# A part of expert 0 computed for all tokens before the routing is known, and another order of the experts

## The chip, the cores and the metric

The kernel runs on one core of a Trainium2 chip. TensorE multiplies matrices, VectorE and ScalarE compute on elements, GpSimd does little here, and SyncE (SP) issues the large transfers from memory, which 16 DMA engines carry. Each engine works through its own instructions in their order and waits for others by semaphores. The metric is device time in microseconds (us) of one execution; the profile takes times within one execution from its first instruction.

## The reference

A network of two layers (gated token mixing, differential attention, pooling; then a feed-forward part), followed by a second network of two layers, on 256 tokens of 1024 numbers. The feed-forward part of layer 1 is a mixture of eight experts, of which each token uses two:

```python
def moe_ffn(x, router_w, w1, w3, w2):
    logits = (xt @ router_w).astype(F32)            # 256 tokens x 8 experts
    top_v, top_i = lax.top_k(logits, TOP_K)         # TOP_K = 2
    top_w = jax.nn.softmax(top_v, axis=-1)
    gates = jnp.sum(jax.nn.one_hot(top_i, N_EXPERTS, dtype=F32) * top_w[..., None], axis=1)
    y = jnp.zeros_like(xt)
    for e in range(N_EXPERTS):
        y = y + gates[:, e:e + 1].astype(x.dtype) * swiglu(xt, w1[e], w3[e], w2[e])
    return y.reshape(bn, s, d)

def swiglu(x, w1, w3, w2):
    return (jax.nn.silu(x @ w1) * (x @ w3)) @ w2    # w1, w3: 1024 x 3584; w2: 3584 x 1024
x = layer_norm(ALPHA * x + f, ln2_g[l], ln2_b[l])   # ahead of it: x = layer_norm(ALPHA * x + h, ln1_g, ln1_b)
```

All is float32. With the inputs that the reference draws, 51, 28, 134, 12, 80, 48, 37 and 122 tokens choose experts 0 to 7.

## The kernel before

Every float32 product is made of three: a number is split into a high part (rounded by ScalarE to fp32r, `wh` for weights) and a low part (the rest, by VectorE, `wl`), and high x high, high x low and low x high are summed in PSUM (`Acc.mm`, L84). Weights come in *units* of 1 MB (128 partitions x 2048): `unit` (L169) takes a landing buffer `raw`, sends the transfer from SP, and splits the tile (`split`, L165) into `wh` and `wl`, of which there are four buffers each. A landing buffer is free again when VectorE has made `wl`. Tokens stand as two tiles of 128; `to_feat` (L313) transposes a tile into the feature-major `xah`, `xal`.

Order: `block1` drains layer 1's mixer, whose end is `project` (L383). Its last three units are multiplied for token tile 0 and then for tile 1; after each tile `layer_norm` (L353) works on VectorE from the two PSUM banks `prj` (r, statistics, aggregate, r, reciprocal of a root from ScalarE, xn). Then comes `moe`: `route` (L805) computes the logits `lgT`, ranks them, counts the tokens of each expert by four products with a matrix of ones (`cum`), sorts the experts by count into *slots* (0 the largest), and leaves the slots' experts in `idi`. A value of it decides a branch on every engine (L1236) between two plans, `few` and `many`; a plan is taken as `few` if slot 0 has up to 192 tokens, slot 1 up to 128 and slot 6 up to 64. Only in the branch does SP know which expert's weights to fetch.

An expert works on gathered tokens: `place` builds one-hot matrices `g`, `gather` (L910) multiplies them with the tokens (32 products `ga`, 256 or 512 columns wide), and the results are copied into `ring`. A full tile holds 128 tokens and needs three products per block of weights, a half tile holds 64 with high and low part side by side and needs two. In the plan `few` the first round takes slots 0 (a full and a half tile), 7 and 6 (half tiles) side by side; slots 1 to 5 follow, one full tile each. For each of seven blocks of 512 inner columns (`f`) an expert takes two units of w1 (`lin`), two of w3, four transposes (`uT`) and two units of w2 (`y`): 42 units. `stream` loads two units ahead. At the end `finish` puts the sum back to the tokens (`sct`) and adds it to the accumulator `xn`.

Instructions are put in order by a scheduler at build time, which also reorders across these calls; what it made stands below.

## Time and profile before

| what | us |
|---|---|
| median of three runs (2356.47 to 2361.75) | 2357.88 |
| the profiled execution | 2355.55 |
| its span, first to last instruction | 2353.8 |
| layer 1's last projection product to the first expert product | 411.5 to 442.0 |
| experts | 442 to about 1450 |

Busy time is a share of the span by engine; TensorE's products are pipelined, so that one lasts 0.39 us by its record while the next begins 0.23 us after it. PEld is the loading of weights into TensorE. The clock is what the chip granted to TensorE, as a share of full speed. The page's second part cuts the span into 40 slices of 58.8 us.

### The profile page before, as it was taken

Reading aid. Unit: us, or ns where it says so; the run is one execution under the profiler, and the core shown is the slowest. Engines: PE = TensorE matmul, PEld = TensorE weight load, DVE = VectorE, ACT = ScalarE, POOL = GpSimd, SP = SyncE. Lnnn points to the kernel's source line nnn. Section 1 sums busy time; section 2 is a strip of 40 time slices with the busy share of each in tenths; the row PEclk is TensorE's granted clock in tenths of the full one; section 3 lists DMA queues with packets and bytes.
Section 4 is the critical chain, followed back from the end, with each engine's and each line's share of the span. In section 5 each row is a group of like instructions: output and inputs, shape, how many; then the busy total and the mean of one; then the engine's idle time right before and its main releaser. Section 6 shows DMA issues by size and latency. Waiting matters only on the chain. (4 is left out here: it accounts for less than half of the span.)

```text
span 2353.8 us, 29770 instructions
## 1 busy us (share of the span) xinstructions
PE 2272.1 (97%) x11444; PEld 1853.7 (79%) x11444; DVE 1765.4 (75%) x1907; ACT 1396.0 (59%) x1532; POOL 108.9 (5%) x154
## 2 busy tenths in 40 slices
PE   7999999799999989999999997999999999999998
PEld 6788887577777768888888886787888888888887
DVE  4665476798888998889888888897666459956653
ACT  5554354677777777676776765457555343764542
POOL 2100011000000000000000001000200001010000
PEclk9999999899999999999999999999999999999999
DMA  9556560699999999999999997643755553555552
GB/s 298 167 191 187 178 209 21 248 343 345 344 337 322 330 326 368 347 368 362 371 342 371 369 365 255 200 162 117 230 190 181 192 189 126 188 172 186 191 185 72
DMA packets 266968, 585.10 MB, mean 249 GB/s; under 512 B 10514, under 2 KB 21190, under 8 KB 266561
## 3 DMA queue, kind: packets, MB, share of 16 engines
q1 hardware_dynamic: 260880, 565.48, 68.4%
q0 software_dynamic: 5936, 17.64, 2.6%
q8 instruction: 91, 1.49, 0.3%
q14 instruction: 61, 0.49, 0.1%
HBM read 580.43 MB, written 2.64 MB: 248 GB/s over the span
## 5 line engine op out<-in xcount | busy, mean ns | idle before, releaser
L167 DVE TENSOR_TENSOR wl<-raw,wh 128x2048 fp32r<-128x2048 f32 (+2 forms) x532 | 1195.5, 2268 | 373.2 <-ACT wh L166 372.1
L166 ACT ACTIVATE wh<-raw 128x2048 fp32r<-128x2048 f32 (+2 forms) x532 | 990.2, 1891 | 383.8 <-PE lin L84 145.3
L950 PE MATMUL lin<-wh,ring 128*128 128x512 f32 x1680 | 556.0, 391 | 0.0
L950 PE MATMUL lin<-wl,ring 128*128 128x512 f32 (+1 forms) x1008 | 396.2, 393 | 3.7 <-DVE wl L167 3.3
L950 PEld LDWEIGHTS lin<-wh,ring 128*128 128x128 f32 x1680 | 315.4, 188 | 81.8
L950 PEld LDWEIGHTS lin<-wl,ring 128*128 128x128 f32 (+1 forms) x1008 | 171.4, 170 | 48.7 <-DVE wl L167 8.5
L84 PE MATMUL lin<-wh,hh 128*128 128x512 f32 x352 | 141.8, 403 | 0.0
L84 PE MATMUL lin<-wl,hh 128*128 128x512 f32 x352 | 138.4, 393 | 2.3 <-DVE wl L167 2.3
L84 PE MATMUL lin<-wh,hl 128*128 128x512 f32 x352 | 137.9, 393 | 0.1
L950 PE MATMUL y<-wl,uh 128*128 128x512 f32 x336 | 107.3, 400 | 3.4 <-DVE wl L167 3.4
L1442 DVE SCALAR_TENSOR_TENSOR ro<-conv,ro 128x256 f32<-128x256 f32 x240 | 105.4, 474 | 0.4
L950 PE MATMUL y<-wh,ul 128*128 128x512 f32 x336 | 104.2, 391 | 0.0
L950 PE MATMUL y<-wh,uh 128*128 128x512 f32 x336 | 104.1, 390 | 0.0
L84 PE MATMUL lin<-wh,h2h 128*128 128x512 f32 x256 | 101.1, 395 | 0.0
L84 PE MATMUL lin<-wl,h2h 128*128 128x512 f32 x256 | 99.9, 390 | 0.2
L84 PE MATMUL lin<-wh,h2l 128*128 128x512 f32 x256 | 99.3, 390 | 0.2
L84 PE MATMUL lin<-wh,xah 128*128 128x512 f32 (+1 forms) x240 | 87.4, 365 | 0.7 <-ACT xah L166 0.6
L84 PE MATMUL lin<-wl,xah 128*128 128x512 f32 (+1 forms) x240 | 86.6, 361 | 0.0
L84 PE MATMUL lin<-wh,xal 128*128 128x512 f32 (+1 forms) x240 | 86.4, 363 | 0.0
L166 ACT ACTIVATE uh<-uT 128x512 fp32r<-128x512 f32 x42 | 25.1, 598 | 99.3 <-PE uT L1004 99.3
L84 PEld LDWEIGHTS lin<-wl,hh 128*128 128x128 f32 x352 | 66.7, 190 | 16.1 <-DVE wl L167 3.2
L84 PEld LDWEIGHTS lin<-wh,hh 128*128 128x128 f32 x352 | 66.8, 190 | 15.6 <-issue 1.3
(548 smaller groups left out, 3812.5 us busy)
## 6 DMA issues: line engine op xcount, KB each, us to landing
raw<-in_moe_w SPq DMA_DIRECT2D x336, 1024.0 KB, 7.2
raw<-in_w_in SPq DMA_DIRECT2D x70, 1024.0 KB, 5.1
raw<-in_w_ff SPq DMA_DIRECT2D x64, 1024.0 KB, 5.2
raw<-in_ffn_w SPq DMA_DIRECT2D x32, 1024.0 KB, 5.1
raw<-in_w_out SPq DMA_DIRECT2D x12, 1024.0 KB, 8.0
raw<-in_w_branch SPq DMA_DIRECT2D x8, 1024.0 KB, 5.7
raw<-in_w_out SPq DMA_DIRECT2D x8, 512.0 KB, 7.4
raw<-in_w_branch SPq DMA_DIRECT2D x8, 512.0 KB, 6.3
```

The source lines that it names most:

```text
L84: nc.tensor.matmul(o, lhsT=lhsT, rhs=rhs, start=(self.i == 0 and self.fresh), stop=(self.i == self.n - 1), skip_group_check=True)
L166: self.nc.scalar.activation(h, src, AF.Copy)
L167: self.nc.vector.tensor_sub(l, src, h.bitcast(F32))
L950: nc.tensor.matmul(a.ap[:rows], lhsT=lhsT, rhs=u[part][:, kk, cs], start=(a.i == 0), stop=(a.i == a.n - 1), skip_group_check=True)
L1442: nc.vector.scalar_tensor_tensor(acc[:, f], uT[:, f, k:k + 256], cw[:, f, k:k + 1], acc[:, f], op0=OP.mult, op1=OP.add)
```

## The change

Expert 0 is taken out of the sorting and goes to slot 0 always; the others are sorted by count into slots 1 to 7. The first block of 512 inner columns of expert 0 is computed for all 256 tokens, without gathering, by a new function `everyone`: six units, below called a0, a1 (w1), b0, b1 (w3), c0, c1 (w2), with 24 products each. a0 is loaded inside the projection (`hook`), the rest in `moe` around the two halves of `route`. The result is added to the accumulator with expert 0's gate, 0 for tokens that did not choose it. Four units of the next block are sent for ahead of the branch (`landed`). Expert 0's other six blocks run on gathered tokens as the plan's first round; slot 1 (full and half tile), 7 and 6 follow, then slots 2 to 5. The bounds for `few` become 128 tokens for expert 0, and 192, 128 and 64 for slots 1, 2 and 6. Six landing buffers go round in a fixed turn, where before every third load took one of the large pool.

```diff
+    def raw(self):
+        if self.raws:
+            self.raws.append(self.raws.pop(0))
+            return self.raws[-1]
+        return self.pw.tile([128, 2048], F32, tag="raw", name="raw")
...
-        raw = (self.big("raw") if self.roomy and self.loads % 3 == 0 else
-               self.pw.tile([128, 2048], F32, tag="raw", name="raw"))
+        there = bool(self.landed)
+        raw = self.landed.pop(0) if there else self.raw()
...
         after[1, 1] = self.early
+        if self.hook:
+            after[0, 0] = self.hook
...
+        key = col(8)
+        nc.vector.tensor_copy(key, cnt)
+        nc.vector.tensor_scalar(key[:, 0:1], cnt[:, 0:1], 1024.0, None, op0=OP.add)
...
+        most = (self.cap, self.cap + 64, self.cap, 64)
+        for i, (slot, m) in enumerate(zip((0, 1, 2, 6), most)):
...
+        def load(name, q):
+            u[name, q] = self.unit(w[name], list(range(4 * q, 4 * q + 4)), 0, 512)
+
+        def up(name, t):
+            x = self.xt_tok(xt)
+            p[name, t] = Acc(self.bank("lin"), 24)
+            for q in range(2):
+                h, l = u[name, q]
+                for kk in range(4):
+                    xh, xl = x(4 * q + kk, t)
+                    p[name, t].mm(nc, xh, h[:, kk])
+                    p[name, t].mm(nc, xh, l[:, kk])
+                    p[name, t].mm(nc, xl, h[:, kk])
+            if name == "a":
+                s[t] = self.mid("sa")
+                nc.scalar.activation(s[t], p[name, t].ap, AF.Silu)
+            else:
+                nc.vector.tensor_mul(s[t], s[t], p[name, t].ap)
...
+        def down(q):
+            h, l = self.unit(w2, [2 * q, 2 * q + 1], 0, 1024)
+            for t in range(2):
+                if q == 0:
+                    y[t] = [Acc(self.bank("y"), 12) for _ in range(2)]
+                for kk in range(2):
+                    uh, ul = (z[:, 2 * q + kk] for z in s[t])
+                    for st, m in ((uh, h), (uh, l), (ul, h)):
+                        for c in range(2):
+                            y[t][c].mm(nc, st, m[:, kk, c * 512:(c + 1) * 512])
...
-        gate, pos, iota, idi = self.route(xt, rw)
+        load, up, turn = (everyone[k] for k in ("load", "up", "turn"))
+        everyone["xt"].extend(xt)
+        self.raws = [*(self.raw() for _ in range(4)), self.big("raw"), self.big("raw")]
+        load("a", 1)
+        up("a", 0)
+        tr1()
+        route = self.route(xt, rw)
+        next(route)
+        load("b", 0)
+        load("b", 1)
+        up("b", 0)
+        up("a", 1)
+        gate, pos, iota, idi = next(route)
...
+        turn(0)
+        up("b", 1)
...
+        turn(1)
+        for q in range(2):
+            everyone["down"](q)
+        for t in range(2):
+            for c in range(2):
+                o = acc[:, t, c * 512:(c + 1) * 512]
+                nc.vector.scalar_tensor_tensor(o, everyone["y"][t][c].ap, gate[t][:, 0:1], o, op0=OP.mult, op1=OP.add)
+        landed = []
+        for w in (w1, w3):
+            for q in range(2):
+                landed.append(self.raw())
+                nc.sync.dma_start(landed[-1].rearrange("p (k n) -> p k n", n=512),
+                                  w[0, 512 * q:512 * q + 512, 512:1024].rearrange("(k p) n -> p k n", p=128))
...
-                for f in range(7):
+                for f in range(es[0][5], 7):
...
+        few = [([(0, 0, False)], [one(0)]),
+               ([(1, 0, False), (1, self.cap, True), (7, 0, True), (6, 0, True)],
+                [[(1, (0, 1), None), (7, (2,), 0), (6, (3,), 1)]]),
+               ([(2, 0, False)], [one(2)]),
+               ([(3, 0, False), (4, 0, False)], [one(3), one(4, 1)]),
+               ([(5, 0, False)], [one(5)])]
```

What the scheduler made of it stands in the next rows, at three places. First VectorE in the norm of token tile 1, from its first bank to the low parts of tile 1. Before:

```order
L363 SCALAR_TENSOR_TENSOR r<-xn,prj 128x512
L365 BN_STATS st<-r 128x6
L167 TENSOR_TENSOR xal<-tr,xah 128x4x128 x2
L363 SCALAR_TENSOR_TENSOR r<-xn,prj 128x512
L167 TENSOR_TENSOR rwhl<-route,rwhl 128x8x8
L365 BN_STATS st<-r 128x6
L366 BN_AGGR mv<-st 128x2
L370 SCALAR_TENSOR_TENSOR r<-r,mv,gb 128x512
L373 RECIPROCAL mv<-mv 128x1
L370 SCALAR_TENSOR_TENSOR r<-r,mv,gb 128x512
L375 SCALAR_TENSOR_TENSOR xn<-r,mv,gb 128x512 x2
```

The same place after the change; the three rows that write wl are the splits of a1, b0 and b1, in this order:

```order
L371 SCALAR_TENSOR_TENSOR r<-xn,prj 128x512
L168 TENSOR_TENSOR wl<-raw,wh 128x2048
L168 TENSOR_TENSOR xal<-tr,xah 128x4x128 x2
L373 BN_STATS st<-r 128x6
L371 SCALAR_TENSOR_TENSOR r<-xn,prj 128x512
L168 TENSOR_TENSOR wl<-raw,wh 128x2048
L373 BN_STATS st<-r 128x6
L168 TENSOR_TENSOR wl<-raw,wh 128x2048
L374 BN_AGGR mv<-st 128x2
L378 SCALAR_TENSOR_TENSOR r<-r,mv,gb 128x512 x2
L381 RECIPROCAL mv<-mv 128x1
L168 TENSOR_TENSOR rwhl<-route,rwhl 128x8x8
```

Three splits of weights now stand inside the norm. Second, TensorE at the four products `cum` that count the tokens of each expert. Before, the last router products stand directly ahead of them:

```order
L839 MATMUL lgT<-xal,rwhl 8x128
L843 MATMUL lgT<-ident,route 128x16
L855 MATMUL cum<-route 128x16
L856 MATMUL cum<-route,one 128x8
L857 MATMUL cum<-route,one 128x8
L858 MATMUL cum<-route,one 128x8
L1234 TENSOR_LOAD idi
L1236 COMPARE_AND_BRANCH
```

After, the end of 48 products of b0, b1 (tile 0) and a0, a1 (tile 1) stands ahead, and the transposes and 24 products of b0, b1 (tile 1) behind:

```order
L84 MATMUL lin<-wh,xah 128x512
L84 MATMUL lin<-wl,xah 128x512
L84 MATMUL lin<-wh,xal 128x512
L869 MATMUL cum<-route 128x16
L870 MATMUL cum<-route,one 128x8
L871 MATMUL cum<-route,one 128x8
L872 MATMUL cum<-route,one 128x8
L1138 MATMUL uT<-ident,sa 128x128 x4
```

The branch of TensorE has moved behind the other 24 products, four transposes and the 48 products of c0 and c1. Third, VectorE at the branch. Before:

```order
L878 TENSOR_TENSOR route<-route 128x64
L879 TENSOR_REDUCE keep<-route 128x8
L1234 TENSOR_LOAD idi
L1236 COMPARE_AND_BRANCH
L1124 TENSOR_SCALAR g<-keep 128x128 x2
L1124 TENSOR_SCALAR g<-keep 128x64 x6
L1146 MEMSET g 128x192 x2
L929 CAST ring<-ga 128x128
```

After, with the adding of the four banks of c0 and c1 to the accumulator (L1186), and then the first gather and the splits of the four units sent for ahead:

```order
L896 TENSOR_REDUCE keep<-route 128x8
L1186 SCALAR_TENSOR_TENSOR xn<-y,keep,xn 128x512 x4
L1331 TENSOR_LOAD idi
L1332 COMPARE_AND_BRANCH
L1219 TENSOR_SCALAR g<-keep 128x128 x2
L1241 MEMSET g 128x128 x2
L950 CAST ring<-ga 128x256
L168 TENSOR_TENSOR wl<-raw,wh 128x2048 x2
L950 CAST ring<-ga 128x256 x3
```

The four additions have come ahead of the branch, and two splits between the first and the other copies of the gather.

## Rows read from the trace of the kernel before

**Rows 1.** The page: TensorE's busy time, and GB/s in the 40 slices.

```profile
PE 2272.1 (97%) x11444; PEld 1853.7 (79%) x11444; DVE 1765.4 (75%) x1907; ACT 1396.0 (59%) x1532; POOL 108.9 (5%) x154
GB/s 298 167 191 187 178 209 21 248 343 345 344 337 322 330 326 368 347 368 362 371 342 371 369 365 255 200 162 117 230 190 181 192 189 126 188 172 186 191 185 72
```

**Rows 2.** Windows: stretch, length, busy by engine, granted clock, DMA share, GB/s.

```profile
core 0: us, PE busy (x) PEld busy (x) DVE busy (x) ACT busy (x) POOL busy (x), PEclk, DMA share, GB/s
411.53:441.97 30.44, 15.63 (x83) 13.25 (x83) 21.57 (x91) 12.46 (x32) 4.20 (x8) 0.72 0.31 110
441.97:811.00 369.03, 360.48 (x1655) 268.11 (x1653) 325.60 (x243) 273.88 (x230) 0.00 (x0) 1.00 0.96 343
811.00:1450.00 639.00, 631.73 (x2883) 517.96 (x2882) 570.53 (x382) 453.40 (x333) 1.09 (x2) 1.00 0.97 354
450.00:460.00 10.00, 10.00 (x45) 7.68 (x44) 7.77 (x5) 7.63 (x7) 0.00 (x0) 1.00 1.04 399
```

**Rows 3.** Groups by form, TensorE, 441.97 to 1450: the largest group.

```profile
L950 PE MATMUL lin<-wh,ring 128*128 128x512 f32 x1680 | 556.0, 391 | 0.0
```

**Rows 4.** The chain that ended last, at 1786 us: start, us, what.

```profile
1786.26 10.90 PE lin L84 x48
1797.15 0.87 PE uT L1824 x8
```

**Rows 5.** Waits of the engines, 1000 to 1400: us in total, times, longest.

```profile
PEld lin L950 <- DVE wl L167: 1.6, 3, 0.5
```

**Rows 6.** Waits of the SP queue, 340 to 1500: us in total, times, longest.

```profile
SPq L191 <- DVE wl L167: 760.4, 303, 25.1
```

**Rows 7.** Timeline of TensorE: start, us, what, [idle before <- what ended it].

```profile
411.30 0.39 PE L84 MATMUL prj<-wh,yl 128*128 128x512 f32 x1
416.16 1.97 PE L320 MATMUL tr<-ident,xn 128*128 128x128 f32 x8 [4.47 <-DVE xn L375]
...
420.81 0.22 PE L839 MATMUL lgT<-xal,rwhl 128*8 128x128 f32 x1
...
433.28 1.19 PE L922 MATMUL ga<-g,xh 128*128 128x512 f32 x2 [7.18 <-DVE g L1146]
...
441.97 0.39 PE L950 MATMUL lin<-wh,ring 128*128 128x512 f32 x1
```

**Rows 8.** Timeline of VectorE in the same stretch.

```profile
411.73 0.69 DVE L363 SCALAR_TENSOR_TENSOR r<-xn,prj 128x512 f32<-128x512 f32 x1 [1.04 <-PE prj L84]
...
415.36 1.41 DVE L375 SCALAR_TENSOR_TENSOR xn<-r,mv,gb 128x512 f32<-128x512 f32 x2
...
426.13 0.17 DVE L862 COPY route<-cum 128x8 f32<-128x8 f32 x1 [1.97 <-PE cum L858]
...
430.73 0.22 DVE L879 TENSOR_REDUCE keep<-route 128x8 f32<-128x64 f32 x1
431.47 1.46 DVE L1124 TENSOR_SCALAR g<-keep 128x128 fp32r<-128x128 f32 x8 [0.52 <-DVE keep L879]
432.91 0.42 DVE L1146 MEMSET g<- 128x192 f32 x2
```

**Rows 9.** Timeline among the experts: additions to the accumulator, and a unit's two splits.

```profile
1105.16 2.72 DVE L1060 SCALAR_TENSOR_TENSOR xn<-sct,keep,xn 128x512 f32<-128x512 f32 x4
...
1112.95 1.92 ACT L166 ACTIVATE wh<-raw 128x2048 fp32r<-128x2048 f32 x1 [0.29 <-PE lin L950]
...
1126.32 2.29 DVE L167 TENSOR_TENSOR wl<-raw,wh 128x2048 fp32r<-128x2048 f32 x1 [1.00 <-ACT wh L166]
```

**Rows 10.** Timeline of ScalarE and TensorE at the end of layer 1's attention.

```profile
390.69 0.60 ACT L657 ACTIVATE aT<-aTp 128x512 f32<-128x512 f32 x1 [3.76 <-PE aTp L655]
391.18 0.59 ACT L166 ACTIVATE yh<-oT 128x512 fp32r<-128x512 f32 x1
...
395.78 0.33 PE L686 MATMUL oT<-ident,o 128*128 128x128 f32 x1 [0.98 <-DVE o L680]
```

**Rows 11.** Timeline of TensorE: a gather 256 columns wide among the experts.

```profile
725.07 0.63 PE L922 MATMUL ga<-g,xh 128*128 128x256 f32 x4
725.54 0.63 PE L922 MATMUL ga<-g,xl 128*128 128x256 f32 x4
```

More of the change, by code (lines that the diff above doesn't have):

```diff
@@ L180, in unit @@
         rv, hv, lv = (z[:, :m].rearrange("p (k n) -> p k n", n=n) for z in (raw, h, l))
-        if layout == "rows":
+        if there:
+            pass
+        elif layout == "rows":
             sv = src[:, c0:c0 + n].rearrange("(g k d) n -> g d k n", g=2, d=64)
@@ L929, in gather, with expert @@
                         nc.vector.tensor_copy(d[1][:, k0:k0 + per], pv[:, :, c0:c0 + n])
-    def expert(self, tiles, w, acc):
+    def expert(self, tiles, w, acc, first):
         nc = self.nc
@@ L1014, in work @@
                         inner = z.get("sum") is not None
-                        if q == 0 and (f == 0 or inner):
-                            st[i]["y"] = [Acc(self.bank("y"), (4 if inner else 28) * per[i]) for c in range(2)]
+                        if q == 0 and (f == first or inner):
+                            st[i]["y"] = [Acc(self.bank("y"), (4 if inner else 28 - 4 * first) * per[i]) for c in range(2)]
                         products(z, st[i][f], (2 * q, 2 * q + 1), u,
@@ L1064, in settle @@
             self.warm(AF.Sqrt, z[:, 0] if tiles[0]["half"] else z[0][:, 0])
-        return up, down, turn, finish, settle
+        return up, down, turn, finish, settle, first
     def stream(self, jobs, ahead=2):
@@ L1087, in stream, with everyone, turn @@
             then()
-    def moe(self, xt, rw, w1, w3, w2, g2, b2):
-        tc, nc = self.tc, self.nc
-        gate, pos, iota, idi = self.route(xt, rw)
+    def everyone(self, w1, w3, w2):
+        nc = self.nc
+        w = {"a": w1, "b": w3}
+        u, p, s, y, xt = {}, {}, {}, {}, []
+        def load(name, q):
[13 more added lines that the diff above has]
+                nc.scalar.activation(s[t], p[name, t].ap, AF.Silu)
+            else:
+                nc.vector.tensor_mul(s[t], s[t], p[name, t].ap)
+        def turn(t):
+            b = self.bank("uT")
+            for j in range(4):
+                nc.tensor.transpose(b[:, j * 128:(j + 1) * 128], s[t][:, j * 128:(j + 1) * 128], self.ident)
+            h, l = self.mid("uh", (128, 4, 128), dt=F32R), self.mid("ul", (128, 4, 128), dt=F32R)
+            self.split(h, l, b.rearrange("p (j c) -> p j c", c=128))
+            s[t] = h, l
+        def down(q):
[8 more added lines that the diff above has]
+                            y[t][c].mm(nc, st, m[:, kk, c * 512:(c + 1) * 512])
+        return dict(first=lambda: load("a", 0), load=load, up=up, turn=turn, down=down, y=y, xt=xt)
@@ L1151, in weights @@
         def weights(s):
+            if s == 0:
+                return [w[0] for w in (w1, w3, w2)]
             rv = index.get(s)
@@ L1216, in make @@
                                     zs[0]["sum"] = ysum[:, inner]
-                                es.append(self.expert(zs, weights(s), acc))
+                                es.append(self.expert(zs, weights(s), acc, int(s == 0)))
                             return es
```

43 lines of the change are left out of this document (22 added, 21 removed).

## Prediction

> **What bounds the kernel now.** I read the page's busy shares and 40 slices first [rows 1]. TensorE is busy for 97% of the span, and one slice stands out in the transfers: the seventh (353 to 412 us) moves 21 GB/s, because nothing of an expert can be fetched before the router has chosen it. The change works at this hole and at the experts behind it, so I cut that part into stretches [rows 2]. From the last product of layer 1's output projection to the first expert product there are 30.4 us, TensorE is busy in half of them, and its granted clock is 0.72. From there to 1450 us TensorE is busy 360.48 of 369.03 us and 631.73 of 639.00 us, at clock 1.00.
>
> Does TensorE really set the pace there, or do the transfers, which run at 343 and 354 GB/s [rows 2]? The experts need 4032 products of 512 columns (12 per full tile and 8 per half tile in each weight unit; the row with 1680 of them is the largest part) [rows 3]. The pitch of such products is 10.90 / 48 = 0.227 us where nothing waits [rows 4]. 4032 x 0.227 = 915 us; with gathers, put-backs, small transposes and 16 us of idle that fills the 1008 us to within 2%. In the 400 us from 1000 to 1400 TensorE's weight loads waited 1.6 us for a split weight [rows 5], while the SP queue held back 303 loads for 760 us until VectorE gave back a landing buffer [rows 6]. So the loads wait for TensorE's progress, not TensorE for the loads: the expert part is TensorE's, and only work that TensorE loses, or idle time that it fills, counts.
>
> **The change, part by part.** The box of before that matters is 411.5 to 442.0 us; all times below are on its clock.
>
> *Work.* With the reference's inputs expert 0 has 51 tokens, so its first 512 inner columns cost 6 units x 12 = 72 products on gathered tokens, and 6 x 24 = 144 for all 256 tokens. That is +72 x 0.227 = +16.3 us of TensorE. The plans: expert 0 stands alone in front, so there is one gather more, 256 columns wide; four of its products take 0.47 us [rows 11], 32 take 3.8 us. Together +20 us of work. The box can pay for it only with its idle and half-speed time: 30.4 us less what its work costs at the full clock (32 gather products 7.3, transposes, router and counts about 4) leaves 19 us. So with no idle left at all the change ends 1 us late; what counts is how much stays idle. I follow the new order through the box.
>
> *Attention's tail.* The split of a0 on ScalarE (1.92 us [rows 9]) now stands ahead of yh and aT. It fits into the 3.76 us gap before aT, but the order of aT and yh is swapped, so aT comes about 1 us later than 390.69, and the 0.98 us that TensorE waits at 395.78 [rows 10] grows by it. End of the projection: 412.6.
>
> *a0 and a1 for tile 0.* They need the feature-major tile 0, whose low part now stands on VectorE behind a1's split: 24 products from 412.9 to 418.3.
>
> *Norm of tile 1.* Before, VectorE takes up the last bank at 411.73 and has the normed tile at 416.77 [rows 8]: 5.0 us. Now a1's split, tile 0's low parts and a statistic keep it until 414.1, and the splits of b0 and b1 (2.29 us each [rows 9]) stand between the two statistics. VectorE: 414.1 + 5.0 + 4.6 and a small split = 424.0. TensorE has nothing to do from 418.3 until the first half is there at 423.3: 5.0 us idle. SiLU's table and the square root's are in front of this root on ScalarE, but they are done before VectorE asks for it.
>
> *Router.* From the normed tile to the last router product before: 416.77 to 421.03, 4.3 us [rows 7, 8], at the lowered clock; I take the same: 428.3. Then 48 products (b for tile 0, a for tile 1), 10.9 us and half a microsecond's wait for a small copy: 439.7. Only here the counts are computed, which took 1.97 us [rows 8]: 441.7; a transpose of 0.44 us [rows 4]; 24 products: 447.6. The counts' whole chain on VectorE (4.8 us before, from 426.13 to 430.95 [rows 8]) is beside this. So is the split of c1, after which the product of SiLU and b for tile 1 (0.7 us) comes: turn at 448.8, then the 48 products of w2: 459.7.
>
> *Branch.* VectorE must add the last two banks to the accumulator before it may branch (0.68 each, 2.72 for four [rows 9]): 461.1. The branch cost it 0.52 us, one-hots for eight and two memsets 1.9 us [rows 8]; for two and two I take 0.8: 462.4. Gather 3.8: 466.2. Behind its first low part stand two weight splits, so the third block's product waits about 1.1 us. The experts start as if at 467.3, where before they started at 441.97 [rows 7]: +25.4 us.
>
> *Behind it.* Expert 0 has 72 products fewer (-16.3), four transposes fewer (-0.4), and the 512-wide gather that stood in the box is now among the experts (+7.3). Same rounds, same six landing buffers, one expert of a kind that ran before. Sum: 25.4 - 16.3 - 0.4 + 7.3 = **+16 us**. On the profiled execution's 2355.55 us (span 2353.8) that is 2371.5; it lies 2.3 us under the median of the three runs, so 2374 against that.
>
> Four loads of the next 512 columns are sent ahead of the branch. I cost them at nothing: they keep the splits supplied from the first product on, but TensorE did not wait for weights at the start before either (10.00 of 10 us busy from 450 to 460 [rows 2]).
>
> Bounds of what before does not show: the idle left in the box lies between 0 (then +1) and, if each wait stands alone and the products behind them run at the lower of the two clock levels (1.2 instead of 2.4 GHz), as the box's mean of 0.72 shows for its 15.6 busy us, +27.
>
> **A rule that speaks against this.** The rows show TensorE busy 98 to 99%, weight loads busy 268 of 369 and 518 of 639 us (73 and 81%), transfers at 343 to 354 GB/s [rows 2]. The Trainium skill (Perfetto Trace Analysis, Identifying the Most-Contended Engine) holds matmul occupancy to be no measure and asks for weight-load busy time and memory utilization instead; its section Engine Utilization gives 358 GB/s as a core's share, which makes 96 to 99% here, with TensorE at 73 to 81%. By that rule the transfers set the pace, and the change wins. Against it the same table has 399 GB/s in one stretch, so the stretches around it were not at a ceiling.
>
> **The rivals.**
> - *The transfers pace the experts.* Ten of 336 loads of 1.05 MB leave the paced part: 10.5 MB at the mean of 350 GB/s [rows 2] = 30 us less. The branch, and with it the first chosen load, moves from 431.9 to about 450.5 (+18.5). Net -11.5: 2346. For it: 343 to 354 GB/s are near a plateau. Against it: the 303 loads that waited for buffers [rows 6] and 1.6 us of waiting at TensorE [rows 5].
> - *The weave is tight.* VectorE lets the norm through before b0's and b1's splits land in its way, the waits at 418 and 460 shrink to 3 us together: +4 to +6, 2362. Against it: VectorE runs its rows in order, and both splits are ahead of the aggregate.
> - *Clock.* The 5 us hole before the router drops TensorE's clock, as the 4.47 us one does before [rows 7], and short waits keep it low for a third of the 144 products: 48 x 0.227 = +11 more, 2385. For it: 0.72 over the box. Against it: 24 and 48 dense products in a row.
> - *It takes the other plan.* If a count missed its bound (expert 0 up to 128 tokens; of the others 192, 128 and 64), four slots would run as two full tiles: 1944 products x 0.227 = +441 us, 2800. The counts (51; 134, 122, 28) leave room.
>
> **How the numbers follow.** Slower by the sum: 0.65, range of its own 2364 to 2382. Tight weave 0.14; clock 0.11; transfers 0.08; other plan 0.02. The likeliest gives **2374**. A change within 0.2% (4.7 us, about what a measurement of this kernel can tell from none) ends at 2362.6: half the tight weave and a little of the main case lie under it. Faster 0.08, same 0.10, slower 0.82. The range takes in the main case, the tight weave's upper half and the start of the clock's: 2362 to 2386; some 0.12 is left out below it and 0.08 above.
>
> **What would show it.** In the profile after: about 55 us from the last projection product to the first product of a gathered tile (30.4 before); a gap of about 5 us before the second set of norm transposes, with VectorE's splits in it; one of about 3 us before the gather, ended by VectorE's one-hots; 0.227 us pitch and 98% busy behind that, so that the expert part is shorter by 9 us. I am wrong if the experts' part shrinks by 25 us or more at a higher transfer rate (the transfers paced it), or if the box takes 45 us or less (the order weaves better than I read it).

## The result, and the profile after

The changed kernel takes 2372.02 us (median of five runs, 2370.46 to 2372.15); five runs of the kernel before have a median of 2357.88 us. The ratio is 1.0055, with a 95% interval of 1.0041 to 1.0070: slower, by 14 us at the medians and 13 by the ratio. The profiled execution has a span of 2370.0 us where the kernel before had 2353.8, so 16.2 us more; the prediction's sum was 16 on that span.

Four marks, found in both timelines of TensorE, cut the two executions into the same stretches: the last product of layer 1's projection (`prj`), the first product of a gathered tile (`lin` from `ring`), the start of the experts' last putting back (`sct`, 1453.54 before, 1470.16 after), and the end. The prediction's 25.4 us up to the first gathered product stand here as 1.1 and 24.3.

| stretch | before, us | after, us | measured change | predicted change |
|---|---|---|---|---|
| to the last `prj` product | 411.30 | 413.96 | +2.66 | +1.1 |
| from there to the first gathered product (the box) | 30.67 | 54.03 | +23.36 | +24.3 |
| from there to the last `sct` | 1011.57 | 1002.17 | -9.40 | -9.4 |
| the rest | 900.26 | 899.84 | -0.42 | 0 |
| span | 2353.8 | 2370.0 | +16.2 | +16 |

First the page of the kernel after, the busy times and the transfer rate in 40 slices, which answers [rows 1] (in all rows PE is TensorE, DVE VectorE, ACT ScalarE and POOL GpSimd):

```profile
PE 2293.1 (97%) x11552; PEld 1871.6 (79%) x11552; DVE 1773.1 (75%) x1920; ACT 1406.5 (59%) x1536; POOL 107.3 (5%) x154
GB/s 303 159 195 180 178 211 105 161 376 302 321 344 341 340 317 351 305 376 349 361 369 364 354 360 292 194 165 116 213 187 179 205 178 128 190 167 194 184 186 74
```

The hole in the transfers has filled from 21 to 105 GB/s, as it was meant to. TensorE is busy for 21 us more. The windows of the kernel after for the box and the experts answer [rows 2] (stretch, length, busy by engine, granted clock, share of the DMA engines, GB/s):

```profile
core 0: us, PE busy (x) PEld busy (x) DVE busy (x) ACT busy (x) POOL busy (x), PEclk, DMA share, GB/s
413.96:467.99 54.03, 46.43 (x237) 38.94 (x235) 35.92 (x86) 23.95 (x27) 5.23 (x8) 0.91 0.38 138
467.99:1470.00 1002.01, 985.05 (x4504) 779.83 (x4502) 885.96 (x643) 720.56 (x571) 1.62 (x4) 1.00 0.95 346
```

Here the change can be read in one line: TensorE is busy 46.43 us of the box, where it was busy 15.63 of 30.44 [rows 2]; the idle time has gone from 14.8 to 7.6 us and the clock has risen from 0.72 to 0.91. The box was filled, with 7 us of idle time and some half-speed time to gain, and the filling cost 31 us more of TensorE's work. Behind it the experts run as before, at 346 GB/s and 98% busy.

TensorE's timeline through the box answers [rows 7] (start, us, what; in brackets the idle time ahead and what ended it):

```profile
413.96 0.39 PE L84 MATMUL prj<-wh,yl 128*128 128x512 f32 x1
...
424.59 1.94 PE L328 MATMUL tr<-ident,xn 128*128 128x128 f32 x8 [4.81 <-DVE xn L383]
...
441.41 0.29 PE L869 MATMUL cum<-route 128*128 128x16 f32 x2
...
449.11 0.66 PE L1138 MATMUL uT<-ident,sa 128*128 128x128 f32 x4 [0.78 <-DVE sa L1133]
...
462.59 0.71 PE L943 MATMUL ga<-g,xh 128*128 128x256 f32 x4 [1.90 <-DVE g L1241]
463.14 0.64 PE L943 MATMUL ga<-g,xl 128*128 128x256 f32 x4
463.62 0.95 PE L943 MATMUL ga<-g,xh 128*128 128x256 f32 x4
464.36 1.05 PE L943 MATMUL ga<-g,xl 128*128 128x256 f32 x4
465.21 1.05 PE L943 MATMUL ga<-g,xh 128*128 128x256 f32 x4
...
467.99 0.40 PE L971 MATMUL lin<-wh,ring 128*128 128x512 f32 x1
```

Only three gaps are left: 4.81 us at the second norm, under a microsecond at the second turn (the transposes `uT`), 1.90 ahead of the gather. VectorE's rows in the same place, which answer [rows 8], tell why the first is there:

```profile
415.35 0.67 DVE L371 SCALAR_TENSOR_TENSOR r<-xn,prj 128x512 f32<-128x512 f32 x1
415.94 3.29 DVE L168 TENSOR_TENSOR wl<-raw,wh 128x2048 fp32r<-128x2048 f32 x1
419.15 0.68 DVE L373 BATCH_NORM_STATS2 st<-r 128x6 f32<-128x512 f32 x1
419.75 2.27 DVE L168 TENSOR_TENSOR wl<-raw,wh 128x2048 fp32r<-128x2048 f32 x1
421.94 0.20 DVE L374 BATCH_NORM_AGGREGATE mv<-st 128x2 f32<-128x12 f32 x1
```

Between the last bank (`r`) and the aggregate (`mv`) stand two splits of weights, those of b0 and b1, 5.6 us together. TensorE had done its 24 dense products by 419.8 and had nothing else that was ready.

### The profile page after: what moved, and what is told of

Same layout as the page of the kernel before. It is cut to its first block, busy times and chain, and to the rows that moved or that the text cites. A ratio compares the mean times of both kernels' runs of the same rounds, so it can differ in the third digit from the quotient of the medians.

```text
span 2370.0 us, 29925 instructions
## 1 busy us (share of the span) xinstructions
PE 2293.1 (97%) x11552; PEld 1871.6 (79%) x11552; DVE 1773.1 (75%) x1920; ACT 1406.5 (59%) x1536; POOL 107.3 (5%) x154
## 3 DMA queue, kind: packets, MB, share of 16 engines
q0 software_dynamic: 5936, 17.64, 2.5%
## 5 line engine op out<-in xcount | busy, mean ns | idle before, releaser
L971 PE MATMUL lin<-wh,ring 128*128 128x512 f32 x1648 | 546.5, 392 | 0.0
L971 PE MATMUL lin<-wl,ring 128*128 128x512 f32 (+1 forms) x992 | 389.5, 393 | 3.2 <-DVE wl L168 3.0
L971 PEld LDWEIGHTS lin<-wh,ring 128*128 128x128 f32 x1648 | 309.3, 188 | 80.8 <-ACT wh L167 0.4
L84 PE MATMUL lin<-wh,xah 128*128 128x512 f32 (+1 forms) x272 | 100.1, 369 | 0.7 <-ACT xah L167 0.6
L84 PE MATMUL lin<-wl,xah 128*128 128x512 f32 (+1 forms) x272 | 99.0, 364 | 0.0
L84 PE MATMUL lin<-wh,xal 128*128 128x512 f32 (+1 forms) x272 | 98.9, 366 | 0.0
L84 PEld LDWEIGHTS lin<-wh,hl 128*128 128x128 f32 x352 | 66.2, 188 | 15.0 <-DVE hl L168 0.9
```

The costliest lines, as they stand in the source:

```text
L84: nc.tensor.matmul(o, lhsT=lhsT, rhs=rhs, start=(self.i == 0 and self.fresh), stop=(self.i == self.n - 1), skip_group_check=True)
L971: nc.tensor.matmul(a.ap[:rows], lhsT=lhsT, rhs=u[part][:, kk, cs], start=(a.i == 0), stop=(a.i == a.n - 1), skip_group_check=True)
```

## The experiments

All kernels are cut at the four marks, since the stretch ahead of the first mark differs from one execution to another (last section). The ratio is to runs of the kernel before on the same chip, with its 95% interval; the change itself was not run again beside the experiments, so it is compared with them by ratios and stretches. The stretches are of one execution each. The five kernels whose experts' part is the same (the change, tile0_only, unwoven, pool_split, norm_first) lie between 1002.05 and 1004.29 us there, so a difference of 2 us in that column says little by itself.

| kernel | to `prj` | box | experts | rest | span | ratio |
|---|---|---|---|---|---|---|
| before | 411.30 | 30.67 | 1011.57 | 900.26 | 2353.8 | 1 |
| the change | 413.96 | 54.03 | 1002.17 | 899.84 | 2370.0 | 1.0055 (1.0041 to 1.0070) |
| half_loads | 416.34 | 32.00 | 1008.80 | 900.06 | 2357.2 | 0.9988 (0.9976 to 0.9999) |
| tile0_only | 414.81 | 39.50 | 1002.19 | 901.80 | 2358.3 | 1.0000 (0.9991 to 1.0010) |
| unwoven | 413.81 | 65.05 | 1003.68 | 901.56 | 2384.1 | 1.0113 (1.0098 to 1.0129) |
| order_only | 411.57 | 26.86 | 1020.35 | 902.42 | 2361.2 | 1.0030 (1.0020 to 1.0040) |
| no_landed | 417.54 | 55.01 | 1006.40 | 901.15 | 2380.1 | 1.0083 (1.0063 to 1.0102) |
| pool_split | 419.67 | 59.66 | 1002.05 | 902.62 | 2384.0 | 1.0095 (1.0081 to 1.0109) |
| norm_first | 417.58 | 53.02 | 1004.29 | 901.31 | 2376.2 | 1.0069 (1.0055 to 1.0082) |
| pair_gather | 413.68 | 54.08 | 1003.70 | 902.64 | 2374.1 | 1.0074 (1.0060 to 1.0087) |
| pair_again | 413.90 | 54.11 | 1000.83 | 901.56 | 2370.4 | 1.0072 (1.0058 to 1.0086) |
| pool_pair | 414.24 | 58.91 | 1006.07 | 900.98 | 2380.2 | 1.0100 (1.0084 to 1.0115) |
| norm_pair | 419.98 | 53.11 | 1002.19 | 904.22 | 2379.5 | 1.0077 (1.0064 to 1.0090) |

**Do the transfers pace the experts?** The kernel before, with half of each expert unit fetched (half_loads):

```diff
-                nc.sync.dma_start(rv[:, i:j], src[ks[i] * 128:(ks[j - 1] + 1) * 128, c0:c0 + n]
+                m2 = (i + j) // 2 if self.roomy else j
+                nc.sync.dma_start(rv[:, i:m2], src[ks[i] * 128:(ks[i] + m2 - i) * 128, c0:c0 + n]
...
+        elif self.roomy:
+            two = lambda z: z.rearrange("p (a n) -> p a n", a=2)
+            self.split(two(h), two(l), raw[:, None, 0:1024].to_broadcast([128, 2, 1024]))
```

> The kernel before, with only the first half of every expert weight unit fetched; both halves of the unit are split from that half, so the experts multiply by half of each unit twice and the output is another one. TensorE's products, ACT's and VectorE's splits stay as many and as large; the bytes of the expert stage fall to about a half. Theory (the products pace the experts, a 512-column product every 0.227 us): 2352 to 2358 us against 2357.9, the first product of the experts at most some us earlier, the expert stage 1006 to 1012 us long. Rival (the transfers pace them, at 343 to 354 GB/s): at least 15 us faster, 2328 to 2343 us, because TensorE's 17 us of idle time in the stage and its pitch both shrink.

Measured: 2356.29 us against 2359.02 of the kernel before on that chip, ratio 0.9988. The experts' window of this kernel:

```profile
448.34:1457.14 1008.80, 994.18 (x4547) 789.28 (x4546) 898.25 (x630) 745.20 (x556) 1.09 (x2) 1.00 0.59 177
```

The rate fell from about 350 to 177 GB/s and the stretch from 1011.57 to 1008.80 us. Half the bytes are worth 2.8 us of 1012: the transfers do not pace the experts, and this is shown, not only read from waits. That the products do is read from TensorE's busy time, 994.18 of the 1008.80 us.

**What do the dense products cost?** The change, with the first block of expert 0 left out for token tile 1 (tile0_only):

```diff
-            for t in range(2):
+            for t in range(1):
...
-        up("a", 1)
...
-        up("b", 1)
...
-        turn(1)
...
-        for t in range(2):
+        for t in range(1):
```

> The changed kernel with the dense part made for the first 128 tokens alone: the first 512 inner columns of expert 0 are left out for the tokens of the second tile, so 72 products fewer (72 x 0.227 = 16.3 us of TensorE) and the output is another one. Theory (in the sum, 144 dense products stand for 72 gathered ones, and nearly all of them lie on the path): most of the 16.3 us comes back and some returns as waits for the selection and for the turn, 2356 to 2361 us, that is about where the kernel before was. Rival (the dense products lie in time in which TensorE would be idle anyway, and the loss has another cause): 2368 to 2372 us.

Measured: 2359.07 us, ratio 1.0000. The box is 39.50 us instead of 54.03, the experts are as long as in the change. So 72 products, 16.3 us of TensorE, are worth 14.5 us of time: nine tenths of them lay on the path. With half of the dense work left undone, the kernel is just as fast as the kernel before, which does all of it.

**Is the weaving worth anything?** The same products, written behind the routing (unwoven):

```diff
-        up("a", 0)
         tr1()
         route = self.route(xt, rw)
...
+        gate, pos, iota, idi = next(route)
+        up("a", 0)
         up("b", 0)
         up("a", 1)
-        gate, pos, iota, idi = next(route)
```

> The changed kernel with the same 144 dense products, the same loads and the same gathers, but with the 24 products of a for tile 0 and the 48 of b for tile 0 and a for tile 1 written behind the whole routing, so that nothing of TensorE's stands inside norm and router. Theory (weaving fills idle time of TensorE, and only that time is worth something; the time between the last projection product and the first gathered product was 30.7 us, of which 14.8 idle, and after the change 54.0, of which 7.6 idle): about 30.7 + 32.7 (144 products) + 3.8 (gather) less the old 512-wide gather's 7.3, less the one-hots' 1.1, plus the waits for the turn and the adds, about 3, is 62 us, so 6 to 12 us slower than the change, 2378 to 2384 us. Rival (the routing's chain on VectorE paces this stretch, and products fit anywhere in it): 2370 to 2374 us.

Measured: 2386.30 us, ratio 1.0113; the box is 65.05 us, 11.0 more than with weaving and 3 more than I had worked out, and the time lies 2 us above my range. TensorE waits in it where it did not:

```profile
424.14 1.97 PE L328 MATMUL tr<-ident,xn 128*128 128x128 f32 x8 [9.95 <-DVE xn L383]
```

The weaving does what it is meant to do, about 11 us of it; it only has to carry more work than that.

**The order of the experts alone.** The change without its dense part; all seven blocks of expert 0 on gathered tokens (order_only):

```diff
-                self.hook = everyone["first"]
+                self.hook = None
...
-        load("a", 1)
-        up("a", 0)
         tr1()
...
-        turn(1)
-        for q in range(2):
-            everyone["down"](q)
...
-                                  w[0, 512 * q:512 * q + 512, 512:1024].rearrange("(k p) n -> p k n", p=128))
+                                  w[0, 512 * q:512 * q + 512, 0:512].rearrange("(k p) n -> p k n", p=128))
...
-                                es.append(self.expert(zs, weights(s), acc, int(s == 0)))
+                                es.append(self.expert(zs, weights(s), acc, 0))
```

> The changed kernel without its dense part: expert 0 is first and the others are sorted, its seven blocks all run on gathered tokens, the four loads ahead of the branch bring the first block's units, nothing is woven into norm and router. Same output as the reference. Theory (the products pace the experts; the order and the loads cost nothing, and a fourth small gather of 3.8 us replaces nothing): 2358 + 3.5 = 2361 us, range 2357 to 2364; so that the dense part is what costs the remaining 11 us of the change. Rival (transfers pace the experts): the four loads that are sent before the branch let everything behind start earlier, 12 us less, about 2347 us.

Measured: 2366.20 us, ratio 1.0030: 7 us slower than before, above my range, and nothing of the 12 us gain of the rival. The box gives 3.8 us back (a 256-wide gather for a 512-wide one, and fewer one-hots), the experts take 8.8 us more, where the 512-wide gather that has moved in accounts for 7.3. The remaining 1.5 us there are idle time of TensorE, 18.3 us instead of 16.8: 0.8 more at turns and 0.6 more in waits for split weights ahead of `y`.

The 2.2 us in the rest begin at the norm behind the experts. Its transposes `tr` start 14.08 us after the last `sct` in the kernel before and 17.64 us after it in order_only; in the change it is 17.43. TensorE in the kernel before, in order_only and in the change:

```profile
1467.62 1.94 PE L320 MATMUL tr<-ident,hn 128*128 128x128 f32 x8 [11.70 <-DVE hn L1261]
1472.32 0.80 PE L84 MATMUL lin<-wl,hh 128*128 128x512 f32 x1 [2.13 <-DVE wl L167]
```

```profile
1476.42 1.94 PE L328 MATMUL tr<-ident,hn 128*128 128x128 f32 x8 [15.26 <-DVE hn L1342]
```

```profile
1487.59 1.94 PE L328 MATMUL tr<-ident,hn 128*128 128x128 f32 x8 [15.05 <-DVE hn L1357]
```

In both new kernels VectorE has two splits of weights among the rows of this norm, where it had none before; these are the change's:

```profile
1481.44 2.28 DVE L168 TENSOR_TENSOR wl<-raw,wh 128x2048 fp32r<-128x2048 f32 x1
...
1483.82 2.24 DVE L168 TENSOR_TENSOR wl<-raw,wh 128x2048 fp32r<-128x2048 f32 x1
```

Behind the transposes some of it comes back, since the kernel before waits 2.13 us there for a split that the new ones have already made: from the transposes to the end it takes 886.18 us before, 884.78 in order_only and 882.41 in the change. So the same thing as in the first norm happens a second time. By the medians the change's loss is thus about half the new order and half the dense part, where I had put a quarter and three quarters.

**The four loads ahead of the branch.** The change without them (no_landed):

```diff
-        for w in (w1, w3):
-            for q in range(2):
-                landed.append(self.raw())
-                nc.sync.dma_start(landed[-1].rearrange("p (k n) -> p k n", n=512),
-                                  w[0, 512 * q:512 * q + 512, 512:1024].rearrange("(k p) n -> p k n", p=128))
```

> The changed kernel without the four loads that are issued ahead of the branch; the first gathered block's units are fetched inside the branch, in the order in which it uses them. Same output as the reference. Theory (their transfers lie beside the dense products and the gather, and the branch's own first loads have the same 13 us of cover; the price in the sum was nothing): 2372 us, range 2369 to 2376. Rival (transfers pace the experts): the stage's first four transfers of some 2.9 us each come later, 12 us slower, 2384 us.

Measured: 2378.92 us, ratio 1.0083. Between my two numbers: box 0.98 and experts 4.23 us longer, so the loads are worth 5.2 us there. Its timeline of TensorE at the first gathered products, and the timeline of ScalarE:

```profile
472.55 0.50 PE L971 MATMUL lin<-wh,ring 128*128 128x512 f32 x1 [0.86 <-ACT wh L167]
474.88 0.50 PE L971 MATMUL lin<-wl,ring 128*128 128x512 f32 x1 [1.83 <-DVE wl L168]
```

```profile
466.96 0.38 ACT L948 ACTIVATE ring<-ga 128x256 fp32r<-128x256 f32 x1 [13.00 <-PE ga L943]
...
470.59 1.91 ACT L167 ACTIVATE wh<-raw 128x2048 fp32r<-128x2048 f32 x1
472.40 0.38 ACT L948 ACTIVATE ring<-ga 128x256 fp32r<-128x256 f32 x1
472.66 5.52 ACT L167 ACTIVATE wh<-raw 128x2048 fp32r<-128x2048 f32 x3
```

The first split now stands among the last copies of the gather, and the first two products wait 2.7 us for the two splits of the first unit. In the change there is no such wait.

It is not the transfer that is late. SP sends for the first unit at 455.71, 16.8 us ahead of the first gathered product (10.1 us in the kernel before, 431.89 to 441.97), and it has landed 5.1 us later, at 460.8. ScalarE is idle from 453.96 to 466.96, but three copies of the gather stand ahead of this split in its order. In the change its splits of the first two landed units stand ahead of the gather:

```profile
451.04 3.73 ACT L167 ACTIVATE wh<-raw 128x2048 fp32r<-128x2048 f32 x2 [0.64 <-DVE idi L910]
```

The kernel before has its first split behind copies of the gather too, but 5.1 us ahead of the first gathered product (441.97), where no_landed has 2.0:

```profile
436.87 1.92 ACT L166 ACTIVATE wh<-raw 128x2048 fp32r<-128x2048 f32 x1
```

**The gap at the norm, first try.** The change, with b0 and b1 split on GpSimd instead of VectorE (pool_split):

```diff
-        self.nc.vector.tensor_sub(l, src, h.bitcast(F32))
+        (self.nc.gpsimd if self.pool else self.nc.vector).tensor_sub(l, src, h.bitcast(F32))
...
+        self.pool = True
         load("b", 0)
         load("b", 1)
+        self.pool = False
```

> The changed kernel with the low parts of b0 and b1 made on GpSimd, so that VectorE's norm rows of token tile 1 stand free of these two splits. Theory (the two splits of VectorE, 3.29 and 2.27 us in the changed kernel, are what TensorE's 4.81 us gap ahead of the second norm transposes consists of, and the gap lies on the path): 4.6 us less, the gap about 0.3 to 1 us, about 2367.5 to 2368.5 us. A GpSimd subtraction of half that size took 2.4 us, so b0 and b1 would be ready some 10 us after the first of them starts, before their products come. Rival (VectorE's rows slow down beside GpSimd, as the split of 3.29 us did, or the products of b wait for GpSimd): no gain, 2371 to 2375 us.

Measured: 2381.47 us, ratio 1.0095, 9 us slower than the change by the medians (the box is 5.6 us longer) and worse than the rival. The gap has grown to 8.73 us. VectorE and GpSimd in this kernel:

```profile
422.73 10.48 DVE L379 SCALAR_TENSOR_TENSOR r<-r,mv,gb 128x512 f32<-128x512 f32 x2
433.14 0.15 DVE L382 RECIPROCAL mv<-mv 128x1 f32<-128x1 f32 x1
```

```profile
418.45 5.38 POOL L169 TENSOR_TENSOR wl<-raw,wh 128x2048 fp32r<-128x2048 f32 x1 [14.52 <-ACT wh L168]
...
425.85 2.35 POOL L1181 TENSOR_TENSOR xl<-xn,xh 128x1024 fp32r<-128x1024 f32 x1
428.15 4.51 POOL L169 TENSOR_TENSOR wl<-raw,wh 128x2048 fp32r<-128x2048 f32 x1
```

Two rows of VectorE that take 0.71 us each in the change took 10.48 us together, and the second ended at 433.2, half a microsecond after GpSimd's last subtraction. The splits had left VectorE's queue and still held VectorE up.

**The gap at the norm, second try.** The two splits stay on VectorE, but behind the norm: one element of each low part is first written from the normed tile (norm_first):

```diff
+        if behind is not None:
+            nc.vector.tensor_copy(l[:, 0:1], behind)
...
-        load("b", 0)
-        load("b", 1)
+        load("b", 0, self.x[:, 1, D - 1:D])
+        load("b", 1, self.x[:, 1, D - 1:D])
```

> The changed kernel with the low parts of b0 and b1 still on VectorE, but held back until token tile 1 is normed: one element of each low part is first written from the normed tile, so that VectorE's two splits stand behind the norm's rows. Theory (the two splits inside the norm are what TensorE waits for in its 4.81 us gap, and that gap lies on the path; the GpSimd variant lost only because VectorE's norm rows stood still beside GpSimd): the gap shrinks to 0 to 1 us; one split then delays the second tile's low parts by about 0.7 us and the other the first copy of the logits by about 2 us, so 1.5 to 3 us less than the change, 2369 to 2371 us, ratio to before about 1.0048. Rival (the routing's chain behind gives all of it back, or the gap has another cause): 2371.5 us or more.

Measured: 2377.23 us, ratio 1.0069; not faster. In the profiled execution 3.6 us of the difference lie ahead of the first mark, so I read the box: 53.02 us instead of 54.03. Its timeline of TensorE:

```profile
423.63 1.23 PE L330 MATMUL tr<-ident,xn 128*128 128x128 f32 x8 [0.21 <-DVE xn L385]
429.13 0.29 PE L852 MATMUL lgT<-xah,rwhl 128*16 128x128 f32 x1 [4.28 <-DVE rwhl L168]
```

The gap of 4.81 us is gone, as expected, and one of 4.28 us has come up 5 us later, ahead of the router's products. VectorE's rows behind the norm:

```profile
424.37 2.29 DVE L168 TENSOR_TENSOR wl<-raw,wh 128x2048 fp32r<-128x2048 f32 x1
426.58 1.28 DVE L168 TENSOR_TENSOR xal<-tr,xah 128x512 fp32r<-128x512 f32 x2
427.78 1.30 DVE L168 TENSOR_TENSOR rwhl<-route,rwhl 128x64 fp32r<-128x64 f32 x1
429.00 2.28 DVE L168 TENSOR_TENSOR wl<-raw,wh 128x2048 fp32r<-128x2048 f32 x1
```

The two splits were indeed what TensorE waited for at the norm; taking them out of it shortens the box by only 1 us. The router's products wait for `rwhl`, the split of the router's weights. In the change it was made inside the norm, at 423.58, in 0.21 us; here it stands behind b0's split and the low parts of the tile, and takes 1.30 us, to the end of a GpSimd subtraction that runs from 426.66 to 429.00. b1's split stands behind it and is not in the gap. An order with `rwhl` and the low parts ahead of both splits was not run, so it is not shown that the gap has to come back.

**One gather less.** Expert 0 and slot 2 placed in one 256-wide gather (pair_gather); its third round's gather lands in one of the four buffers that slot 1 still uses, so the output is another one. In pair_again the rounds stand in another order and this does not happen:

```diff
-        few = [([(0, 0, False)], [one(0)]),
+        few = [([(0, 0, False), (2, 0, False)], [one(0), one(2, 1)]),
+               ([(3, 0, False), (4, 0, False)], [one(3), one(4, 1)]),
                ([(1, 0, False), (1, self.cap, True), (7, 0, True), (6, 0, True)],
                 [[(1, (0, 1), None), (7, (2,), 0), (6, (3,), 1)]]),
-               ([(2, 0, False)], [one(2)]),
-               ([(3, 0, False), (4, 0, False)], [one(3), one(4, 1)]),
```

> The changed kernel with expert 0 and the second slot of one full tile placed and gathered together (columns 0 to 127 and 128 to 255 of one 256-wide gather), so that the experts need one 256-wide gather less. Theory (TensorE paces the experts and a gather of 32 products of 256 columns costs 3.8 us): 2372 - 3.8 = about 2368.5 us, range 2367 to 2371. Rival (the gather lies in time in which TensorE would wait for splits anyway): 2371 to 2374 us.

> The changed kernel with expert 0 and slot 2 in one 256-wide gather, as in the earlier pairing, but with slots 3 and 4 as the next round and slots 1, 7 and 6 behind them, so that no gather lands in one of the four buffers that the running round still reads. Same output as the reference. Theory (one gather of 32 products less is worth its TensorE time, 3.8 us in the sum, 2.7 us of busy time by the earlier pairing, whose gain was eaten by waits for a gather buffer): 2368 to 2370 us, ratio about 1.0045. Rival (the gathers' copies on ScalarE and VectorE, not TensorE's products, set what a gather costs, and they are as many as before): 2371 to 2374 us.

Measured: 2375.76 us, ratio 1.0074, and 2374.85 us, ratio 1.0072. Neither gains. The experts' window of pair_again:

```profile
468.01:1468.84 1000.83, 981.39 (x4473) 775.88 (x4471) 884.65 (x639) 718.01 (x569) 4.82 (x10) 1.00 0.96 346
```

TensorE is busy 3.66 us less, almost exactly the price of the gather in the sum, but the stretch is only 1.34 us shorter: its idle time has grown from 17.1 to 19.4 us, by 1.3 us of waits for split weights and 0.9 us at turns. (norm_pair against norm_first, the same edit, has 2.1 us.) The norm behind the experts then starts its transposes 1.4 us later after the `sct` row than in the change, which takes what was left. Both edits together, with the one and with the other place for the splits (pool_pair and norm_pair):

> Both edits at once: b0 and b1 split on GpSimd, and expert 0 gathered together with the second one-tile slot. Theory (both lie on the path and add up): 2372 - 4.6 - 3.8 = about 2364 us, range 2362 to 2367; still slower than the kernel before, 2358 to 2359 us. Rival (either of the two is hidden): 2368 to 2373 us.

> Both: b0's and b1's low parts behind the norm, and expert 0 gathered together with slot 2 in the new order of rounds. Same output as the reference. Theory (both lie on the path and add): 2365 to 2368 us, ratio about 1.0035, still slower than the kernel before. Rival: no more than one of them counts, 2369 to 2372 us.

Measured: 2382.11 and 2377.19 us, ratios 1.0100 and 1.0077. The two terms do not add; neither came out by itself either. (The output of pool_pair is another one, as that of pair_gather, from whose order of rounds it is made.)

No experiment points to a version that beats the kernel before: with half of the dense part left out the change ties with it, and what was meant to mend the rest moved waits without removing them.

## Why the prediction was right

The prediction holds: slower, by the mechanism that it gave most chance, 2 us under the predicted time. That the span came within 0.2 us of the sum is in part luck: attention's tail took 1.6 us more than worked out and the box 0.9 less, and the rest, set at nothing, is a sum of two errors. Point by point:

- **The bound.** Right, and half_loads shows it as far as the transfers go. The rival of the transfers falls with it, and so does what the prediction drew from the rule of the Trainium skill (Perfetto Trace Analysis, Identifying the Most-Contended Engine): by weight-load busy time and memory utilization the transfers stood at 96 to 99% of the core's share and TensorE at 73 to 81%, yet halving the bytes moved the time by 0.1%. The measurement decides. The share was no ceiling here: the Trainium skill (Perfetto Trace Analysis, Engine Utilization) gives it for both cores of a pair at work and says that one active core can pull more, and the trace agrees, with 399 GB/s over 10 us [rows 2]. What idle time TensorE has among the experts is mostly waits for split weights, 12.1 of 16.8 us before (8.8 ahead of `y`, 3.3 ahead of `lin`); the 1.6 us that the prediction read hold for 1000 to 1400 us alone.
- **Work: 144 products for 72.** Right. tile0_only took 72 of them away and the box shrank by 14.5 of their 16.3 us; the experts' part is shorter by 9.40 us, where the sum had -16.3 - 0.4 + 7.3 = -9.4.
- **Attention's tail, +1.1 us.** Mis-sized in the first table, +2.66, but not in its mechanism. ScalarE's rows of the kernel after answer [rows 10]: a0's split stands ahead and `aT` starts at 391.75, 1.06 us later than before.

```profile
388.33 1.91 ACT L167 ACTIVATE wh<-raw 128x2048 fp32r<-128x2048 f32 x1 [1.22 <-PE prj L84]
391.25 0.60 ACT L167 ACTIVATE yh<-oT 128x512 fp32r<-128x512 f32 x1 [1.01 <-PE oT L696]
391.75 0.59 ACT L667 ACTIVATE aT<-aTp 128x512 f32<-128x512 f32 x1
```

  The other 1.6 us come behind it, from `aT` to the last projection product: 22.21 us in the change, 20.61 before. In pool_pair, which has the same a0 there, it is 20.58 us. The difference is the clock, 0.92 in the change and 1.00 in pool_pair over these stretches: the ten products `o` took 2.34 us in the change and 1.28 in pool_pair.

```profile
393.24 2.34 PE L677 MATMUL o<-vo,aT 128*128 128x128 f32 x10
```

```profile
394.61 1.28 PE L678 MATMUL o<-vo,aT 128*128 128x128 f32 x10
```

  These are the change's row and then pool_pair's. So the step of the order was worth 1 us as worked out, and a fall to the lower clock level came on top, which no row of before had shown.
- **The norm's gap, 5.0 us.** Right in size (4.81) and cause. Its words that both splits stand between the two statistics do not fit the rows: b1's stands behind the second; both are ahead of the aggregate, so the sum is the same. What the prediction did not say, norm_first showed: the gap is one place where VectorE's backlog shows, and with the splits behind the norm a wait comes up at the router, b0's split being 2.3 of its 4.28 us.
- **Counts, turn and products.** The 48 products ended 1.7 us later than worked out (441.4 against 439.7), 1.6 of which the tail had brought; the counts cost 0.8 us of TensorE instead of 1.97, at a granted clock of 1.00 (0.62 before, from 420 to 430), and the second turn came at 449.1 where I had 448.8. Errors of 1 to 2 us with opposite signs.
- **Branch and gather.** The gather started at 462.59 (I had 462.4), behind a gap of 1.90 us ended by VectorE's rows for `g`, where I said about 3. It took 5.4 us instead of 3.8: from the third piece on a piece took up to 1.05 us instead of 0.64, at half the clock (0.50 from 464 to 467). The kernel before had shown this: its gather in the box took 8.7 us (433.28 to 441.97 [rows 7]) where the sum has 7.3. The 1.1 us that I had set down for a wait on the splits was not there. That the two errors nearly cancel is luck.
- **The landed loads, costed at nothing.** Right in the number, not in its reason. There is no wait at the first gathered products, as before. But that there was none before either does not carry over: without the loads the change waits, and loses 5.2 us (no_landed). There the loads of the branch have 16.8 us up to the first gathered product, more than the 10.1 us before. What is missing is a place for their splits: ScalarE starts the first one 9.8 us after its unit has landed, behind three copies of the gather and 2.0 us ahead of the first gathered product, where it was 5.1 us before.
- **The gather's price of 3.8 us among the experts.** As TensorE's busy time right (3.66 in pair_again), as time only 1.3 to 2.1, which is within the spread of that stretch. I had let every product among the experts count in full; with 17 us of idle time in that stretch a part of the work removed comes back as waiting.
- **The rest, at nothing.** Measured -0.42, but as a sum: the norm behind the experts gives TensorE its transposes 3.4 us later, with two splits among its rows, and 3.8 us come back behind it, 2.1 of them a wait of the kernel before that is gone. The prediction looked at the splits in the first norm and not in this one.
- **The rivals.** Tight weave: no, the box took 54 us; the wait at 418 is 4.81 and the one at 460 is 1.90. Lower clock: beyond the router, where the sum had it, it did strike twice, in attention's tail (1.6 us) and in the gather (1.6 us), not in the 144 products, whose box has a clock of 0.91. Other plan: not taken.

What stays open: what another order of `rwhl` and the splits would give back at the router; 1.6 of the 3.8 us that come back behind the experts; and what sets the place where the clock falls.

## What to carry to other kernels

Before filling idle time with work that will be done twice over, write down the idle time and the work side by side: here 14.8 us of idle time, of which filling won back 7 to 11, stood against 31 us of extra products that saved 16 later. A gap ahead of one instruction of the busy engine is worth its length only if the engine that ends it has nothing else to do before the next one; otherwise the wait moves on. And data that has landed is not yet data that can be used: where a split stands between the two, its place in the order of its engine decides, and a change that shortens the work around it can bring up a wait that the profile before did not have.

## What the runs showed of the hardware

**A VectorE instruction with two operands in SBUF, the on-chip memory of the tiles, stands still while GpSimd subtracts.** In pool_split a VectorE instruction that takes 0.71 us took 8.91 us, and one 1.65 us, beside GpSimd's subtractions of two operands in SBUF; in the change itself one split took 3.29 us instead of 2.28 beside one, and in norm_first `rwhl` 1.30 instead of 0.21. A row that takes one of its operands from PSUM went on at its pace: `r` from `xn` and `prj` took 0.67 us at 421.06 in pool_split, beside the first subtraction. The two instructions of that line in pool_split (shortest, median and longest in ns, first and last start):

```profile
L379 DVE SCALAR_TENSOR_TENSOR r<-r,mv,gb x2: 1651/5280/8909, 422.7 to 424.3; 128x512 f32<-128x512 f32 x2
```

The Trainium skill (SBUF — State Buffer, SBUF: two separate sides) states it: VectorE with two inputs in SBUF and GpSimd share a pair of ports as an exclusive lock, and the loser waits for the whole instruction. The trace agrees, and shows that the wait can go on over two GpSimd instructions one behind the other. The row that stood from 424.3 did so 1.5 us ahead of the first of these two, while GpSimd issued three transfers (423.78 to 425.84); why it did not get through there is not shown. Moving work from VectorE to GpSimd to free VectorE does the opposite for such instructions.

**The clock does not fall at the same place in each execution.** In attention's tail, whose code is the same in the kernels here except for a0, the granted clock of 360 to 405 us was 1.00 in the kernel before, 0.96 in the change and 0.89 in norm_first:

```profile
360.00:405.00 45.00, 40.85 (x236) 30.08 (x235) 27.98 (x61) 22.47 (x65) 5.12 (x7) 1.00 0.10 27
```

```profile
360.00:405.00 45.00, 39.99 (x225) 29.50 (x224) 28.50 (x59) 24.45 (x66) 5.12 (x7) 0.96 0.36 120
```

```profile
360.00:405.00 45.00, 40.49 (x220) 28.46 (x220) 27.44 (x58) 23.50 (x65) 5.12 (x7) 0.89 0.37 120
```

These are three kernels, in that order. TensorE works there in short bursts with waits of 1 to 2 us between them. The last projection product came at 411.3 to 411.6 us where the clock was 1.00 without a0 (before, order_only), at 413.7 to 414.8 where it was 0.96 (the change and four others with a0), and at 416.3 to 420.0 where it was 0.89 (half_loads without a0, four others with it). Up to there half_loads and the kernel before are written alike, and show 0.89 and 1.00. That is several times the effects of the last experiments, so they are read from stretches behind this one and not from a difference of medians.
